# Seven pairs of gates in seven half-size products ahead of the branch steps of a decoder layer

## The chip, the cores and the metric

The kernel runs on one core of one Trainium2 chip. The metric is device time in microseconds of one execution, the median of several. Before the change it is 1901.4 us (three runs, 1900.49 to 1901.96). A core has five engines that run side by side, each with its own queue of instructions in a fixed order: PE (matmul), DVE (vector), ACT (activation), POOL and SP, which here only issues DMAs. A matmul of this kernel takes weights of 128x128 and a moving operand of 128x512; PSUM holds eight accumulators of 128x512.

## The reference, cut to what matters

One decoder layer over 1024 tokens of width 1024, float32. The part around the change:

```
u = x * (1.0 + scale_m) + shift_m
proj = jnp.einsum('btd,de->bte', u, w_in)
...
qa, ka, va, qb, kb, vb, ga, gb = jnp.split(proj, offs, axis=-1)
...
ya = jnp.einsum('bte,ed->btd', oa.reshape(Bn, T, A_Q_W), w_branch_a)
yb = jnp.einsum('bte,ed->btd', ob.reshape(Bn, T, B_OUT_W), w_branch_b)
merged = jax.nn.sigmoid(ga) * ya + jax.nn.sigmoid(gb) * yb
return jnp.einsum('btd,de->bte', merged, w_o)
```

`oa` and `ob` are the outputs of two attentions. `scale_m`, `shift_m` and four more vectors come from `silu(c)` times `w_ada` (the adaLN work). A normalisation, a SwiGLU feed-forward (FFN) and a second normalisation follow.

## The kernel before, in words

Everything is held with features on partitions, in chunks of 128. Matmul operands are split in a high and a low part (`split`, L116: ACT copies to a rounded format, DVE subtracts), and each product is made of three matmuls, high x high, high x low, low x high (`mac`, L136, lines 137 to 139). Each engine issues its instructions in the order in which the program emits them (L107), so a waiting instruction holds all that are queued behind it on its engine.

- **u**, the modulated input, is kept split in eight tiles of `bigu` (L127 to 133): for each part, token half t and half of the features.
- **Weights** come through `class Weights` (L41): three raw pieces of 128x512 loaded ahead by SP, split into four pairs of buffers; `take` hands out pieces in the order of `add`, `prepare` and `step` split the next ones.
- **Phase 1** (to L776): projections of u and the two attentions, interleaved. Two gate chunks, `tail_gates` (L149), are made at its end and written to `ga_d` (L697 to 700). Attention outputs go to `oa_d` (eight tiles of 128x1024, the last one by POOL's queue, L618 to 625) and `ob_d`.
- **Branch phase** (L781 to 915). The order is written out in `order` (L159 to 164): 24 branch steps, three branches of eight chunks, each step 24 matmuls from four attention parts; and the 14 remaining gates, each 48 matmuls from u (`make_gate`, L850): one ahead of step 0, which belongs to step 8, and then one ahead of each step from 8 to 22, save those made early, which are only loaded. `o_parts` (L804) loads four attention parts through two buffers and splits them, at the gates ahead of steps 0, 8 and 16. `merge` (L863) puts a step's result in `merged`: ACT copies in branch 0, DVE adds and POOL multiplies by the gate in branch 1, DVE multiplies and POOL adds in branch 2. `split_merged` splits the result for the output projection.
- **adaLN work**: `ada_steps` (L815) is a generator that is advanced by one at each branch step and three or four times in each gate. It makes the vectors 2, 3, 4 and 5: for each, eight rows of `w_ada` are loaded (512 KB each) and summed on DVE (L824, L826), then some matmuls with ones finish it (L835 or L842).
- **FFN** (from L1039): the first product of gate and up weights is made as seven half-size products per pair of chunks (Strassen's scheme): operands `b11`, `b21`, `t2`, `t1`, `t3`, `b22`, `t4` are sums and differences of blocks of the input, and the weights' sums are made on POOL (`g_sums`, L1073). `product` (L1100, matmuls at L1106) is 12 matmuls. The first two products of three pairs need only `b11` and `b21`, and run while the other operands are being made (`late_input`, L1149).

Of the kernel before, what the change touches and what calls it, by code (L numbers as in the profile page):

```python
# [10 lines left out]
F32 = mybir.dt.float32  # L11
# [7 lines left out]
P = 128  # L19
# [77 lines left out]

@with_exitstack
def decoder_layer(ctx: ExitStack, tc: tile.TileContext, I, out, dbg=None):
# [27 lines left out]
    def wide(name, pool, halves=(0, 1)):  # L127

        ts = {(s, t, k): pool.tile([P, 4, TH], F32R, name=f"{name}{s}{t}{k}", tag="big")
              for t in halves for k in range(2) for s in range(2)}  # L130
        return lambda s, t, k: ts[s, t, k // 4][:, k % 4]

    u = wide("u", bigu)
# [18 lines left out]
    for dc in tail_gates:  # L152
        add_chunk(I["w_in"][46 + dc], 2, 4)
    steps = [(b, dc) for b in range(3) for dc in range(KC)]
    gate_of = {8 + dc: 46 + dc for dc in range(KC)}
    gate_of.update({16 + dc: 54 + dc for dc in range(KC)})
    branch_w = [I["w_branch_a"][0], I["w_branch_a"][1], I["w_branch_b"]]
    made_early = [8 + dc for dc in tail_gates]
    order = []  # L159
    for i in range(len(steps)):  # L160
        g = 8 if i == 0 else i + 1
        if g in gate_of and i != 7:
            order.append(("g", g))
        order.append(("w", i))
    for kind, i in order:
        if kind == "g" and i not in made_early:
            add_chunk(I["w_in"][gate_of[i]], 2, 4)
        elif kind == "w":
            b, dc = steps[i]
            add_chunk(branch_w[b][dc], 1, 4)  # L170
# [37 lines left out]
    oa_d = dram.tile([A_PAIRS, P, T], F32, name="oa_d")  # L208
    ob_d = dram.tile([B_PAIRS, P, T], F32, name="ob_d")
    ga_d = dram.tile([KC, P, T], F32, name="ga_d")  # L210
# [7 lines left out]
    with tc.tile_pool(name="pro", bufs=2) as pro:  # L218
# [38 lines left out]
        def modulate(j):  # L257
            mod = pro.tile([P, 2], F32, name="mod", bufs=3)
# [521 lines left out]

    zp = ctx.enter_context(tc.tile_pool(name="zp", bufs=2, side="right", reuse_waits="tile"))  # L781
    misc = ctx.enter_context(tc.tile_pool(name="misc", bufs=1, side="right", reuse_waits="tile"))
    pools["low"] = low = ctx.enter_context(tc.tile_pool(name="low", bufs=6, reuse_waits="tile"))
    ph2b = ExitStack()
    mix = ph2b.enter_context(tc.tile_pool(name="mix", bufs=2, reuse_waits="tile"))
# [18 lines left out]
    def o_parts(b):  # L804
        parts = []
        for k in range(4):
            send_parts(4 * b + 4)
            hl = low.tile([P, 2, T], F32R, name="o_hl", tag="big")
            split(hl[:, 0], hl[:, 1], o_raws.pop(0))
            parts.append(hl)  # L810
        return parts

    shsc = misc.tile([P, 2, KC], F32, name="shsc")

    def ada_steps():  # L815
        for m in (2, 3, 4, 5):
            acc = mix.tile([P, T], F32, name="acc", bufs=1)
            raws = {}
            for k in range(KC + 1):
                if k < KC:  # L820
                    raws[k] = mix.tile([P, T], F32, name="a_raw", bufs=2)
                    nc.sync.dma_start(raws[k], I["w_ada"][k * P:(k + 1) * P, m * D:(m + 1) * D])
                if k == 1:
                    nc.vector.tensor_scalar(acc, raws[0], c_act[:, 0:1], None, op0=OP.mult)  # L824
                elif k > 1:
                    nc.vector.scalar_tensor_tensor(acc, raws[k - 1], c_act[:, k - 1:k], acc, op0=OP.mult, op1=OP.add)  # L826
                yield
            yield
            if m in (2, 5):
                gt = (mix if m == 2 else misc).tile([P, T], F32, name=f"gate{m}", bufs=1)  # L830
                nc.sync.dma_start(gt, I["b_ada"][:, m * D:(m + 1) * D].to_broadcast([P, D]))
                for t in range(2):
                    s = slice(t * TH, (t + 1) * TH)
                    ps = ps_2.tile([P, TH], F32, name="p2")
                    nc.tensor.matmul(ps, ones, acc[:, s], start=True, stop=True)  # L835
                    nc.vector.tensor_tensor(gt[:, s], ps, gt[:, s], op=OP.add)
                nc.vector.tensor_scalar(gt, gt, 1.0, None, op0=OP.add)
                gates[m] = gt
            else:
                ps = ps_2.tile([P, TH], F32, name="p2")  # L840
                for k in range(KC):
                    nc.tensor.matmul(ps[:, k:k + 1], acc[:, k * P:(k + 1) * P], ones[:, :1], start=True, stop=True)  # L842
                nc.vector.tensor_tensor(shsc[:, m - 3], ps[:, :KC], b_pp[:, m * 8:m * 8 + 8], op=OP.add)
                if m == 4:
                    nc.vector.tensor_scalar(shsc[:, 1], shsc[:, 1], 1.0, None, op0=OP.add)

    ada = ada_steps()
    gts = {}

    def make_gate(i, *steps):  # L850
        g = mix.tile([P, T], F32, name="gt", bufs=2)
        gts[i] = g
        if i in made_early:
            nc.sync.dma_start(g, ga_d[i - 8])
            return
        ps = [ps_2.tile([P, TH], F32, name="p2") for _ in range(2)]
        for n, t in enumerate(gemm_u(ps, ws.take(2), *steps)):
            if n % 4 == 2:
                next(ada, None)
            if t is not None:  # L860
                sigmoid_half(g[:, t * TH:(t + 1) * TH], ps[t])
# [551 lines left out]
```

## Time and profile before

| what | value |
|---|---|
| median of three runs | 1901.4 us |
| the profiled execution, its own time | 1908.77 us |
| its span, first to last instruction | 1907.0 us |
| granted TensorE clock over the span | 0.987 |
| gates and branches, from the first gate matmul to the output projection | 819.80 to 1122.24 us |
| gate matmuls (`p<-u`) in this stretch | 3 x 224 |
| branch matmuls (`p<-o_hl`) in this stretch | 3 x 192 |
| adaLN sums on DVE, L826 | x28, 1323 ns each |
| half-size products of the FFN, L1106 | 21 groups of 88 matmuls, the first at 1217.4 us |

The page gives busy time by engine, a strip of 40 slices, the DMA queues and the costliest groups of instructions. In a group's line stand line, engine, operation, the written and read tiles by name, the shape, the count; then busy us and mean ns of one; then the idle time of the engine just before them and what ended it. Matmuls are pipelined, so that their durations overlap. A row of windows gives for one stretch each engine's busy time with the count of its instructions, then granted clock, DMA share and GB/s. A row of the timeline gives start, duration, engine, line and, in brackets, the engine's idle time before it and what released it.

### The profile page before, as it was taken

The page shows a single profiled execution, that of the slowest core. Times are in us where ns is not written, and L with a number is a line of the kernel's source. Part 1 is how long each engine was busy: PE and PEld are TensorE (multiplying, and loading weights), DVE is VectorE, ACT ScalarE, POOL GpSimd, SP SyncE. Part 2 cuts the span into 40 slices and gives each one's busy share as a digit, 9 for nine tenths or more (in the row PEclk, how much of TensorE's full clock was granted, in tenths as well). Part 3 has the DMA queues.
Part 4 walks back from the last instruction along what each step waited for, and adds up shares of the span by engine and source line. Part 5 has one row for each costly group of instructions (what it writes and reads, how often), then busy time and mean ns, then how long its engine had stood idle before and what let it go on. Part 6 is the DMA issues. An engine that isn't in the chain of part 4 may idle for free.

```text
span 1907.0 us, 24471 instructions
## 1 busy us (share of the span) xinstructions
PE 1841.1 (97%) x8988; PEld 1489.6 (78%) x8988; DVE 1160.4 (61%) x2161; ACT 782.0 (41%) x1661; POOL 596.5 (31%) x389
## 2 busy tenths in 40 slices
PE   6899999999999999989999999999999999899998
PEld 5688877878878777768888878778888888788886
DVE  7855667667677887534555364575565444565557
ACT  3455545445444767633122132653333333412122
POOL 2432223223323222100311142455664333431213
PEclk9899999999999999989999999999999999999999
DMA  8011112111121122254534123123222222432222
GB/s 316 28 34 34 40 41 74 45 57 56 41 63 50 53 89 68 79 178 164 175 118 161 56 75 124 56 89 100 89 78 89 78 89 95 135 125 90 93 71 89
DMA packets 72266, 170.83 MB, mean 90 GB/s; under 512 B 13073, under 2 KB 14161, under 8 KB 72146
## 3 DMA queue, kind: packets, MB, share of 16 engines
q1 hardware_dynamic: 71810, 168.21, 26.7%
q8 instruction: 71, 1.16, 0.3%
q0 software_dynamic: 336, 1.06, 0.2%
q14 instruction: 49, 0.40, 0.1%
HBM read 145.80 MB, written 23.43 MB: 89 GB/s over the span
## 4 chain that ended last, share of the span: by engine, by line
PE 51%; DVE 3%; ACT 1%; issue 1%; DMA 1%; SPq 0%; POOL 0%; DVEq 0%; ACTq 0%; POOLq 0%
PE pf L1106 21%; PE p L138 5%; PE p L139 5%; PE p L137 5%; PE pf L137 5%; PE pf L139 5%; PE pf L138 5%; DVE m L118 1%; DMA h_raw<-h_d 0%; DVE wd L79 0%; DVE h L118 0%; DMA oa_d<-o 0%; PE px L1034 0%; PE p L835 0%; PE p L842 0%
## 5 line engine op out<-in xcount | busy, mean ns | idle before, releaser
L137 PE MATMUL pj<-u,w_hi 128*128 128x512 f32 x720 | 301.5, 419 | 0.0
L139 PE MATMUL pj<-u,w_lo 128*128 128x512 f32 x720 | 283.9, 394 | 0.0
L138 PE MATMUL pj<-u,w_hi 128*128 128x512 f32 x720 | 282.6, 392 | 0.0
L425 POOL TENSOR_TENSOR rb<-rb,sin_t 128x512 f32<-128x512 f32 x64 | 86.8, 1356 | 502.0 <-DVE rb L423 431.5
L118 DVE TENSOR_TENSOR w_lo<-r,w_hi 128x512 fp32r<-128x512 f32 x110 | 117.7, 1072 | 138.7 <-ACT w_hi L117 137.9
L79 DVE TENSOR_TENSOR w_lo<-w_raw,w_hi 128x512 fp32r<-128x512 f32 x150 | 133.4, 893 | 85.3 <-ACT w_hi L78 83.0
L528 ACT ACTIVATE probs<-probs,st 128x128 f32<-128x128 f32 (+1 forms) x320 | 146.0, 461 | 60.5 <-DVE st L518 30.8
L137 PEld LDWEIGHTS pj<-u,w_hi 128*128 128x128 f32 x720 | 136.4, 189 | 33.6 <-issue 4.7
L139 PEld LDWEIGHTS pj<-u,w_lo 128*128 128x128 f32 x720 | 135.8, 189 | 30.7
L138 PEld LDWEIGHTS pj<-u,w_hi 128*128 128x128 f32 x720 | 136.7, 190 | 22.6
L137 PE MATMUL pf<-wd,h 128*128 128x512 f32 x352 | 139.2, 395 | 3.4 <-DVE zt L1326 2.9
L138 PE MATMUL pf<-wd,h 128*128 128x512 f32 x352 | 138.7, 394 | 1.9 <-DVE wd L79 1.9
L139 PE MATMUL pf<-wd,h 128*128 128x512 f32 x352 | 138.6, 394 | 0.0
L62 POOL TENSOR_TENSOR w_raw<-w_raw,gate 128x512 f32<-128x512 f32 x60 | 83.1, 1404 | 157.0 <-DMA w_raw<-in_w_down 134.4
L1326 DVE SCALAR_TENSOR_TENSOR zt<-zt,pf 128x512 f32<-128x512 f32 x112 | 76.2, 685 | 85.1 <-PE pf L139 85.0
L426 POOL TENSOR_TENSOR r<-ra,rb 128x512 f32<-128x512 f32 x63 | 114.5, 1817 | 6.1 <-DVE kl L460 1.3
L78 ACT ACTIVATE w_hi<-w_raw 128x512 fp32r<-128x512 f32 x150 | 92.0, 624 | 29.0 <-PE p L138 12.0
L552 ACT ACTIVATE ptsb<-pt 128x512 f32<-128x512 f32 (+1 forms) x128 | 63.6, 548 | 93.6 <-PE pt L550 93.2
L137 PE MATMUL p<-u,w_hi 128*128 128x512 f32 x224 | 88.3, 394 | 0.0
L139 PE MATMUL p<-u,w_lo 128*128 128x512 f32 x224 | 87.2, 389 | 0.0
L138 PE MATMUL p<-u,w_hi 128*128 128x512 f32 x224 | 87.2, 389 | 0.0
L137 PE MATMUL p<-o_hl,w_hi 128*128 128x512 f32 x192 | 75.9, 395 | 8.0 <-ACT o_hl L117 8.0
(297 smaller groups left out, 4267.2 us busy)
## 6 DMA issues: line engine op xcount, KB each, us to landing
w_raw<-in_w_in SPq DMA_DIRECT2D x118, 256.0 KB
r<-in_w_gate_up SPq DMA_DIRECT2D x47, 512.0 KB
a_raw<-in_w_ada SPq DMA_DIRECT2D x32, 512.0 KB
w_raw<-in_w_down SPq DMA_DIRECT2D x44, 256.0 KB
h_raw<-h_d SPq DMA_DIRECT2D x22, 512.0 KB
h_d<-g SPq DMA_DIRECT2D x40, 256.0 KB
wa<-in_w_ada_m SPq DMA_DIRECT2D x16, 512.0 KB
wb<-wt_d SPq DMA_DIRECT2D x24, 256.0 KB
```

What stands on the lines that cost most here:

```text
L62: self.nc.gpsimd.tensor_tensor(self.raws[i], self.raws[i], scale(), op=OP.mult)
L78: self.nc.scalar.activation(hi, raw, AF.Copy)
L79: self.nc.vector.tensor_tensor(lo, raw, hi, op=OP.subtract)
L118: nc.vector.tensor_tensor(lo, src, hi, op=OP.subtract)
L137: nc.tensor.matmul(ps, w[0], m[0], start=first, stop=False)
L138: nc.tensor.matmul(ps, w[0], m[1], start=False, stop=False)
L139: nc.tensor.matmul(ps, w[1], m[0], start=False, stop=last)
L425: eng.tensor_tensor(b, b, sin_t[:, s], op=OP.mult)
L426: eng.tensor_tensor(residue_half(res, r, t), by_residue(a, r), by_residue(b, r), op=OP.add)
L528: nc.scalar.activation(pr, pr, AF.Exp, bias=st[:, 0, h, b:b + 1], accum_out=st[:, 1, h, b:b + 1])
L1106: nc.tensor.matmul(ps, w[:, c], m[:, k], start=first and k == 0 and n == 0, stop=k == 3 and n == 2, skip_group_check=True)
L1326: nc.vector.scalar_tensor_tensor(z, z, ALPHA if gi == 0 else 1.0, pd, op0=OP.mult, op1=OP.add)
```

## The change

The 14 gates leave the branch steps. A phase of their own follows phase 1 and precedes all branch steps:

- The 14 gate chunks form seven pairs, each computed by the FFN's scheme in seven products of 12 matmuls. The FFN's helpers become a class, `SevenProducts`, which both phases use.
- `b11`, `b21` and `b22` are tiles of u that exist already. `t1`, `t2`, `t3` and `t4` need differences in float32, so the input is loaded again (`u_load`, 1 MB for each of four slices), scaled again on ACT with the vectors that are now kept in `mods`, subtracted on POOL and DVE, and split (`u_differences`).
- The first two products of four pairs run first. Their weights: those of pairs 0 and 1 through `Weights`, those of pairs 2 and 3 by a load of their own. Then come the other products of those pairs and the three remaining pairs.
- Each gate is put together from the products on ACT, DVE and POOL, goes through the sigmoid and is written to `ga_d`; the branch steps load all 16 gates from there.
- Of the adaLN work the vectors 3 and 4 (22 advances of the generator) are made in this phase, 2 and 5 in the branch steps.
- In the branch steps the attention parts of the next branch are loaded and split one by one at steps 3 to 6 of the branch before, branch 1's into `bigu`; those of branch 0 are all loaded and split ahead of step 0. `merged` is split one chunk a step from step 17 on. `oa_d` becomes eight tensors.

The core of the diff:

```diff
-        add_chunk(I["w_in"][gate_of[i]], 2, 4)
+    for p in range(2):
+        add_chunk(I["w_in"][pairs[p][0]], 2, 4)
...
+    def product(self, ps, i, first):
+        hi, lo = self.ready.pop(0)
+        b = self.B[PRODUCTS[i]]
+        for k in range(4):
+            c = slice(k * P, (k + 1) * P)
+            for n, (w, m) in enumerate(((hi, b[0]), (hi, b[1]), (lo, b[0]))):
+                self.nc.tensor.matmul(ps, w[:, c], m[:, k], start=first and k == 0 and n == 0,
+                                      stop=k == 3 and n == 2, skip_group_check=True)
...
+    def u_load(k):
+        again[k] = [row(), row()]
+        for x_t, j in zip(again[k], (k, k + 4)):
+            nc.sync.dma_start(x_t, I["xT"][j])
+
+    def u_differences(k):
+        ua, ub = again.pop(k)
+        for x_t, j in ((ua, k), (ub, k + 4)):
+            nc.scalar.activation(x_t, x_t, AF.Identity, bias=mods[:, j, 0:1], scale=mods[:, j, 1:2])
+        t3 = raw_t3[k // 2][:, (k % 2) * TH:(k % 2 + 1) * TH]
+        nc.gpsimd.tensor_tensor(t3, ub[:, t_half], ua[:, t_half], op=OP.subtract)
+        nc.vector.tensor_tensor(ua[:, t_half], ua[:, t_half], ua[:, :TH], op=OP.subtract)
+        nc.vector.tensor_tensor(ua[:, :TH], ub[:, t_half], ua[:, t_half], op=OP.subtract)
+        nc.vector.tensor_tensor(ub[:, :TH], ub[:, :TH], ua[:, :TH], op=OP.subtract)
+        for name, src in (("t2", ua[:, :TH]), ("t1", ua[:, t_half]), ("t4", ub[:, :TH])):
+            split_to(name, k, src)
...
+    def first_quarter(p):
+        dst = out_half(pairs[p][0], 0)
+        nc.scalar.activation(dst, acc[p][0], AF.Copy)
+        nc.vector.tensor_tensor(dst, dst, acc[p][1], op=OP.add)
+        gate_out(pairs[p][0], 0)
+
+    ws.prepare(4)
+    for got in ws.done[ws.used:ws.used + 4]:
+        gat.ready.append(got[:2])
+    ws.used += 4
+    u_load(0)
+    for p in (2, 3):
+        gat.load(p, False)
+    u_load(1)
+    for p in range(EARLY_GATES):
+        acc[p] = [ps_2.tile([P, TH], F32, name="p2") for _ in range(2)]
+        for i in range(2):
+            gat.product(acc[p][i], i, True)
+            if p < 2:
+                gat.split(2 + p, i)
+        u_differences(p)
+        if p + 2 < 4:
+            u_load(p + 2)
+        if p < 2:
+            gat.load(p)
+        first_quarter(p)
+        if p == 2:
+            for step in range(3):
+                gat.sums(0, step)
+    operand("t3", bigu)
+    gat.jobs = [(p, i) for p in range(len(pairs)) for i in range(2 if p < EARLY_GATES else 0, 7)]
+    gat.prepare(2)
+    for k in range(4):
+        split_to("t3", k, raw_t3[k // 2][:, (k % 2) * TH:(k % 2 + 1) * TH])
...
+    send_parts(2)
...
+    for k in range(4):
+        o_part(0, k)
+    for i, (b, dc) in enumerate(steps):
+        w = ws.take(1)
...
+        if b < 2 and dc >= 3 and dc < 7:
+            o_part(b + 1, dc - 3)
+        if i + 1 >= 8 and i + 1 < len(steps):
+            make_gate(i + 1)
```

Here `gate_out` is the sigmoid (ACT tanh, then a scaling on DVE) and, once both halves are done, the write to `ga_d`; `make_gate` is now only the load; `o_part` splits one attention part and has the next one loaded.

More of the change, by code (lines that the diff above doesn't have):

```diff
@@ new lines, in decoder_layer @@
+    again = {}
+    def u_load(k):
[13 more added lines that the diff above has]
+            split_to(name, k, src)
@@ new lines, in mrg, with send_parts, o_part @@
+    def mrg(dc, t):
+        return merged[dc // 4][:, dc % 4, t * TH:(t + 1) * TH]
+    o_src = [oa_d[p] for p in range(A_PAIRS)] + [ob_d[p] for p in range(B_PAIRS)]
+    o_raws, o_sent = [], [0]
+    def send_parts(upto):
+        while o_sent[0] < min(upto, len(o_src)) and len(o_raws) < 2:
+            raw = mix.tile([P, T], F32, name="o_raw", bufs=2)
+            nc.sync.dma_start(raw, o_src[o_sent[0]])
+            o_raws.append(raw)
+            o_sent[0] += 1
+    parts_of = {}
+    def o_part(b, k):
+        send_parts(4 * b + k + 1)
+        hl = (bigu if b == 1 else low).tile([P, 2, T], F32R, name="o_hl", tag="big")
+        split(hl[:, 0], hl[:, 1], o_raws.pop(0))
+        parts_of.setdefault(b, []).append(hl)
+        send_parts(len(o_src))
@@ L848, in decoder_layer, with make_gate @@
     gts = {}
-    def make_gate(i, *steps):
+    def make_gate(i):
         g = mix.tile([P, T], F32, name="gt", bufs=2)
         gts[i] = g
[L853 to L861, printed above, removed]
+        nc.sync.dma_start(g, ga_d[i - 8])
```

277 lines of the change are left out of this document (149 added, 128 removed).

## The prediction

> **What bounds the kernel now.** I read the page first, then the stage between the last tail gate and the output projection by windows, then its PE groups, then single instructions.
>
> ```profile
> span 1907.0 us, 24471 instructions
> PE 1841.1 (97%) x8988; PEld 1489.6 (78%) x8988; DVE 1160.4 (61%) x2161; ACT 782.0 (41%) x1661; POOL 596.5 (31%) x389
> ```
>
> The profiled execution's own time is 1908.8 us, 7.4 above the median of 1901.4; I work out a difference in the profile and apply it to the median. About 0.2% (4 us) is what a measurement of this kernel can tell from no change.
>
> ```profile
> core 0: us, PE busy (x) PEld busy (x) DVE busy (x) ACT busy (x) POOL busy (x), PEclk, DMA share, GB/s
> 819.80:830.77 10.97, 10.97 (x49) 9.10 (x50) 3.04 (x5) 2.89 (x5) 1.72 (x3) 1.00 0.87 280
> 830.77:886.52 55.75, 46.94 (x194) 37.65 (x192) 18.91 (x21) 16.80 (x28) 2.95 (x2) 0.91 0.47 161
> 886.52:1122.24 235.72, 235.72 (x1050) 194.30 (x1048) 118.82 (x147) 51.87 (x89) 51.52 (x32) 1.00 0.37 122
> 1260.00:1640.00 380.00, 380.00 (x1678) 314.74 (x1678) 205.51 (x222) 147.46 (x263) 188.07 (x121) 1.00 0.27 90
> 822.00:830.00 8.00, 8.00 (x37) 6.63 (x36) 1.27 (x2) 1.06 (x1) 1.03 (x2) 1.00 0.97 298
> ```
>
> ```profile
> L137 PE MATMUL p<-u,w_hi 128*128 128x512 f32 x224 | 88.3, 394 | 0.0
> L137 PE MATMUL p<-o_hl,w_hi 128*128 128x512 f32 x192 | 75.9, 395 | 8.0 <-ACT o_hl L117 8.0
> ```
>
> The first window is one gate, the second the eight steps of branch 0, the third everything else up to the projection, the fourth the FFN's seven-product phase, which runs for 380 us without a hole. PE is the bound in all of them. A matmul lasts 394 ns, but these overlap: 380.00 us over 1678 is **0.2265 us from start to start**, and that, not 394 ns, is what a removed matmul is worth. Eight branch steps are 192 matmuls, 43.5 us at that spacing, and took 55.75: 12.3 us are lost in branch 0 before.
>
> ```profile
> 842.32 0.80 PE L137 MATMUL p<-o_hl,w_hi 128*128 128x512 f32 x1 [8.00 <-ACT o_hl L117]
> 843.58 0.80 PE L138 MATMUL p<-o_hl,w_hi 128*128 128x512 f32 x1 [0.46 <-DVE o_hl L118]
> 845.03 0.63 PE L138 MATMUL p<-o_hl,w_hi 128*128 128x512 f32 x1
> 845.45 0.63 PE L139 MATMUL p<-o_hl,w_lo 128*128 128x512 f32 x1
> 848.39 0.39 PE L137 MATMUL p<-o_hl,w_hi 128*128 128x512 f32 x1
> ```
>
> That loss is one hole of 8.0 us (the third and fourth attention part come late), and then matmuls 0.42 us apart until 848.39: from 843.58 on eleven distances from start to start take 4.81 us where 2.49 are due. So a long hole costs 2.3 us more after it ends. The granted clock of the window, 0.91, shows the same.
>
> **The products.** Fourteen gates are 224 x 3 = 672 matmuls of 128x512. Seven pairs in seven products of 12 are 588 of the same shape. 84 fewer at 0.2265 us: **-19.0 us**. The adaLN matmuls and the 576 of the branches stay.
>
> The Trainium skill, "TensorE: Matmul & The Clock Gate", section "Back-to-back issue gap", gives about 131 ns for each matmul in a sustained stream of load-and-matmul pairs at 512 columns; by that the 84 would be worth 11.0 us, an estimate. The window of 380 us disagrees, and the measurement decides.
>
> **The old hole.** Branch 0 now comes more than 130 us after the attention's last write, so that write can no longer hold it: **-12.3 us**.
>
> **The early gates.** The new phase opens with 8 products that need only the old u: 96 matmuls, 21.7 us, from 819.8 to 841.5. Then PE needs t2, all four slices, and the weights of pair 0's third product. Those hang on a chain through ACT, DVE and POOL, each in the order of emission. Per slice k: two scalings of 128x1024 on ACT; POOL subtracts for t3; DVE may overwrite that half of x only after POOL has read it, then makes three differences, each from the one before; ACT writes three high parts, DVE three low parts; then the gate's first quarter: ACT copy, DVE add, ACT tanh. The next slice's scaling is queued on ACT behind that tanh, so slices don't overlap.
>
> ```profile
> L265 ACT ACTIVATE ut<-xt,mod x9: 802/1239/1247, 11.3 to 64.2; 128x1024 f32<-128x1024 f32 x7, 128x512 f32<-128x512 f32 x2
> L1047 POOL TENSOR_TENSOR b11l<-raw,b11h x4: 1293/1298/1303, 1202.2 to 1209.9; 128x512 fp32r<-128x512 f32 x4
> L1163 POOL TENSOR_TENSOR r<-r x3: 1807/1810/1814, 1225.6 to 1233.6; 128x512 f32<-128x512 f32 x3
> L1155 DVE TENSOR_TENSOR raw<-r,raw x3: 677/678/692, 1224.7 to 1232.7; 128x512 f32<-128x512 f32 x3
> L1156 DVE TENSOR_TENSOR raw_t<-r,raw x3: 691/692/693, 1225.5 to 1233.5; 128x512 f32<-128x512 f32 x3
> L1047 DVE TENSOR_TENSOR t2l<-raw_t,t2h x4: 999/1002/1003, 1226.9 to 1239.2; 128x512 fp32r<-128x512 f32 x4
> L1047 DVE TENSOR_TENSOR t1l<-raw,t1h x4: 677/678/679, 1231.5 to 1240.7; 128x512 fp32r<-128x512 f32 x4
> ```
>
> ```profile
> L78 ACT ACTIVATE w_hi<-w_raw 128x512 fp32r<-128x512 f32 x150 | 92.0, 624 | 29.0 <-PE p L138 12.0 <-POOL w_raw L62 10.9 <-PE p L139 5.5
> L681 ACT ACTIVATE gt<-p 128x512 f32<-128x512 f32 x28 | 16.5, 596 | 154.6 <-PE p L139 136.1 <-issue 9.3 <-DVE acc L826 9.2
> L1260 DVE TENSOR_TENSOR g<-g,pf 128x512 f32<-128x512 f32 x40 | 27.5, 687 | 15.5 <-PE pf L1106 15.5
> ```
>
> Scalings 2.4 (two of 1.24, slightly overlapped), POOL 1.3 (1.8 where DVE works beside it), two differences with hand-over 1.4, three high parts from there on 1.7 (the third difference lies beneath), last low part 0.8, add 0.7, tanh 0.6: 8.9, with the hops **9.0 us per slice**. Between 8.5 and 10.
>
> Where it starts: SP sends the tail gate's result, two branch weights, x^T for slice 0 (1 MB), then the first half-weights of pairs 2 and 3. ACT's next job is the split of pair 2's, queued ahead of slice 0.
>
> ```profile
> 821.25 1.72 SPq L800 DMA_DIRECT2D o_raw<-oa_d  x2
> ```
>
> ```profile
> 827.82 1.06 ACT L117 ACTIVATE o_hl<-o_raw 128x1024 fp32r<-128x1024 f32 x1 [6.44 <-DMA o_raw<-oa_d]
> 830.53 1.06 ACT L117 ACTIVATE o_hl<-o_raw 128x1024 fp32r<-128x1024 f32 x1 [1.64 <-DMA o_raw<-oa_d]
> ```
>
> ```profile
> 833.86 2.35 POOL L624 TENSOR_TENSOR o<-o,vt 128x1024 f32<-128x1024 f32 x1 [7.49 <-issue]
> 836.50 0.60 POOL L625 DMA_DIRECT2D oa_d<-o  x1 [0.30 <-POOL o L624]
> ```
>
> In the same place 1 MB issued at 821.25 was in by 830.5, with the DMA 97% busy at 298 GB/s. I take 830.5 for pair 2's weights (828 to 834: half a MB more is queued ahead, but the engines stay full from 823 on). Two splits, 1.1: slice 0 at 831.6. POOL isn't free then: it still has attention's last pair (L624, L625) until 837.1, where slice 0 wants it at 834: +3.2. Slice 0 ends at 843.8. Only behind it stand pair 3's two splits on ACT (1.1), so pair 3's products wait too, from 836.5 to about 845, inside the longer wait. Slices 1 to 3: 27.0, and 1.5 for POOL's weight sums beside slice 2's DVE work (1.0 against 0.68 above): 873.4. Then pair 0's split, 0.6: **PE goes on at 874.0 instead of 841.5: +32.5**, and 2.3 for the cold clock: **+34.8**. With the bounds of start (-2.5 to +3.5), slice (-2 to +4) and POOL (-3 to +3): 27 to 43.
>
> **The steady gates** copy the FFN's scheme, which holds 0.2265 us. They add three adaLN steps a pair on DVE; DVE is 54% busy in the FFN's window (205.51 of 380) with the same splits. I cost this at nothing, up to 3.
>
> **Into the branches.** Before, a gate's 10.97 us covered the first splits and the step's weights were split ahead of them. Now nothing does. After the last product ends: ACT copy and tanh 1.2, DVE scaling 0.4, and only then can SP pass the write of that gate and issue the first two attention parts.
>
> ```profile
> 847.00 0.43 SPq L822 DMA_DIRECT2D a_raw<-in_w_ada  x1
> ```
>
> ```profile
> 850.92 1.28 DVE L826 SCALAR_TENSOR_TENSOR acc<-a_raw,c_act,acc 128x1024 f32<-128x1024 f32 x1 [0.49 <-DMA a_raw<-in_w_ada]
> ```
>
> ```profile
> L117 ACT ACTIVATE o_hl<-o_raw 128x1024 fp32r<-128x1024 f32 x12 | 12.4, 1054 | 31.6 <-DMA o_raw<-oa_d 14.0 <-DMA oa_d<-o 9.6 <-DMA o_raw<-ob_d 8.0
> L118 DVE TENSOR_TENSOR o_hl<-o_raw,o_hl 128x1024 fp32r<-128x1024 f32 x12 | 14.4, 1222 | 28.5 <-ACT o_hl L117 28.5
> ```
>
> ```profile
> L682 DVE TENSOR_SCALAR gt<-gt x28: 418/426/428, 844.6 to 1112.2; 128x512 f32<-128x512 f32 x28
> ```
>
> A load of 512 KB takes 3.9 us from issue (847.00) to landing (850.92). Issue about 2.6 after the last product, with the gate's 512 KB ahead of it: part 0 in at 6.8, split by 9.1 (1.05 + 1.22). There are two buffers, so parts 2 and 3 are issued at 9.1 and 10.2 and land at 13.0 and 14.1; part 3's high half is done at 15.2. The step's own weights are split behind all four parts: high at 15.8, low at 17.1. PE has the adaLN's matmuls until about 1.7 and then nothing until 15.8: 14.1 idle, about 0.8 more for the low weights, 2.3 cold clock: **+17.2** (12 if the loads land faster, 20 if a buffer is still held).
>
> The second half of the branches lose their gate matmuls as cover. A step is 24 matmuls, 5.44 us; DVE per step in branch 2: weights 0.7, two products from PSUM 1.4, adaLN 1.28, two low parts of the merged rows 1.4 to 2: 4.8 to 5.4. Just beneath PE; cost nothing, up to 4.
>
> **Sum**: -19.0 - 12.3 + 34.8 + 17.2 = **+20.7 us**; 1901.4 becomes **1922.1**.
>
> On the clock the same page of the Trainium skill ("What's actually happening") says that the array falls to half rate after an idle window of some 3.4 us and recovers after as long a busy one, which speaks against both new holes. By it each would cost 1.7 us, an estimate; the trace agrees on half rate (0.42 against 0.2265), at 2.3.
>
> **Rivals.**
> Not slower: the differences hide beneath the early products. Place: the same four slices; it decides at PE's return. If t2 and its weights are there by 853.3 instead of 874.0, the change is even. The FFN's similar slices start 4.0 us apart (L1155: 1224.7 to 1232.7 for three); four of those from 831.6, with POOL free at once, end at 847.6 and PE returns at 848.2: 6.7 lost and 2.3 for the clock in place of 34.8, so -19.0 - 12.3 + 9.0 + 17.2 = -5.1: 1896. For it: the FFN builds the same t operands with little loss. Against: there the scalings come out of PE, and no first quarter stands between the slices. Chance 0.13. Half of that effect gives no change: 0.06.
> Worse: the DMA becomes the bound in steps 8 to 15. They load 8 weights of 256 KB, 8 gates, 8 adaLN rows and 4 attention parts of 512 KB, 12.6 MB in 43.5 us, 290 GB/s; the busiest row shows 298. It decides below 290: at 240 these steps take 52 us, and the whole is +29: 1930. Against: loads are issued ahead by two buffers. Chance 0.10.
>
> **How the numbers follow.** The forecast has 0.71; its bounds (27 to 43, 12 to 20, 0 to 7) give 1909 to 1940. The range reaches down to 1903 for the even case and to 1938: it leaves out most of the faster rival and the tail. Faster 0.13, same 0.06, slower 0.81.
>
> **What would show it.** Right: a hole of about 20 us on PE ahead of the first t2 product, ended by ACT or DVE of w_hi and w_lo; slices 9 us apart on ACT; a shorter hole ahead of pair 3's products; 588 gate matmuls at 0.2265; a hole of about 14 us ahead of the first branch product, ended by the branch weights' split; no hole in branch 0 from attention's last write; the FFN unchanged. Wrong: PE back before 853, the branch hole under 8 us, or holes inside steps 8 to 15 ended by loads.

## The result, and the profile after

| | before | after |
|---|---|---|
| median of three runs | 1901.4 us (1900.49 to 1901.96) | **1943.81 us** (1942.89 to 1945.09) |
| ratio of the times, 95% interval | | 1.0225 [1.0209, 1.0241] |
| span of the profiled execution | 1907.0 us | 1942.0 us |
| granted TensorE clock over the span | 0.987 | 0.977 |

The change makes the kernel 42.4 us slower. The forecast was 20.7 us slower with a range up to 1938: the sign was right, the size was half of it, and the time lies above the range.

The head of the page of after:

```profile
span 1942.0 us, 24554 instructions
PE 1827.4 (94%) x8904; PEld 1475.2 (76%) x8904; DVE 1228.0 (63%) x2224; ACT 834.3 (43%) x1741; POOL 651.7 (34%) x428
```

PE has 84 instructions and 13.7 us of busy time less than before, and yet the span is longer: the time is in holes. Windows of both kernels, by stage, place it. First before: gates and branches, output projection, the FFN's products.

```profile
819.80:1122.24 302.44, 293.63 (x1290) 241.04 (x1290) 140.78 (x173) 71.55 (x120) 56.19 (x37) 0.98 0.41 135
1122.24:1168.39 46.15, 43.98 (x194) 35.80 (x192) 28.46 (x31) 12.89 (x20) 23.06 (x17) 1.00 0.36 113
1217.44:1648.32 430.88, 426.73 (x1881) 351.74 (x1880) 246.75 (x280) 181.26 (x319) 214.93 (x137) 0.99 0.26 87
```

Then the same three stages of after:

```profile
818.07:1159.27 341.20, 284.25 (x1206) 229.50 (x1206) 210.57 (x240) 124.94 (x202) 110.40 (x75) 0.91 0.53 181
1159.27:1209.36 50.09, 46.80 (x194) 37.92 (x192) 26.27 (x27) 12.14 (x19) 24.63 (x17) 0.93 0.31 104
1258.30:1688.34 430.04, 426.30 (x1882) 351.63 (x1880) 246.87 (x280) 181.28 (x319) 213.09 (x135) 0.99 0.26 87
```

Gates and branches take 38.8 us more, the output projection 3.9 us more, the FFN nothing. The span grew by 35.0 us only, less than the 42.4 of the medians: the profiled execution of before was itself 7.4 us above its median, and 5.0 of that lie behind the FFN's products, in work that the change doesn't touch (258.69 us against 253.71 after). Inside the first stage, windows of the early gates up to the first product on t2, the other gates, and the branches:

```profile
818.07:878.01 59.94, 26.10 (x97) 20.03 (x97) 27.38 (x41) 24.99 (x37) 14.28 (x12) 0.74 0.48 167
878.01:1017.01 139.00, 119.24 (x524) 97.87 (x525) 86.58 (x102) 61.09 (x105) 48.31 (x32) 0.93 0.49 167
1017.01:1159.27 142.26, 138.91 (x585) 111.60 (x585) 96.60 (x99) 38.85 (x62) 47.81 (x31) 0.97 0.59 199
```

In the first of these PE does 96 matmuls, worth 21.7 us, in 59.94. The PE rows of the timeline at the end of each larger hole say what ended it:

```profile
832.41 0.73 PE L153 MATMUL p<-u,w_hi 128*128 128x512 f32 x2 [3.19 <-ACT w_hi L176]
846.79 1.22 PE L153 MATMUL p<-u,w_hi 128*128 128x512 f32 x2 [6.79 <-ACT w_hi L176]
878.01 0.79 PE L153 MATMUL p<-t2h,w_hi 128*128 128x512 f32 x1 [23.87 <-ACT w_hi L176]
...
918.03 0.50 PE L153 MATMUL p<-t3h,w_lo 128*128 128x512 f32 x1 [4.86 <-DVE w_lo L177]
...
1017.01 0.80 PE L198 MATMUL p<-o_hl,w_hi 128*128 128x512 f32 x1 [13.94 <-ACT w_hi L78]
1152.52 0.50 PE L200 MATMUL p<-o_hl,w_lo 128*128 128x512 f32 x1 [2.58 <-DVE w_lo L79]
1168.65 0.79 PE L199 MATMUL p<-w_lo,m 128*128 128x512 f32 x1 [2.74 <-DVE w_lo L79]
```

The first three are the early gates (33.9 us), and the fifth is the entry into the branches: both stages were forecast to wait. The fourth, inside the gate loop, and the last two, in branch 2 and the output projection, were not.

### The profile page after: what moved, and what is told of

Read it like the earlier page. It is cut to its first block, busy times and chain, and to the rows that moved or that the text cites. A ratio compares the mean times of both kernels' runs of the same rounds, so it can differ in the third digit from the quotient of the medians.

```text
span 1942.0 us, 24554 instructions
## 1 busy us (share of the span) xinstructions
PE 1827.4 (94%) x8904; PEld 1475.2 (76%) x8904; DVE 1228.0 (63%) x2224; ACT 834.3 (43%) x1741; POOL 651.7 (34%) x428
## 4 chain that ended last, share of the span: by engine, by line
PE 44%; DVE 5%; DMA 2%; ACT 1%; issue 1%; POOL 0%; SPq 0%; DVEq 0%; POOLq 0%; ACTq 0%
PE pf L153 21%; PE p L153 5%; PE pf L198 5%; PE pf L199 4%; PE pf L200 4%; PE p L200 2%; PE p L199 2%; PE p L198 2%; DVE m L177 1%; DMA gate<-in_b_ada 1%; DVE w_lo L79 1%; DVE acc L864 1%; DMA a_raw<-in_w_ada 1%; DMA o_raw<-oa_d 1%; DMA h_raw<-h_d 0%
## 5 line engine op out<-in xcount | busy, mean ns | idle before, releaser
L177 DVE TENSOR_TENSOR w_lo<-r,w_hi 128x512 fp32r<-128x512 f32 x141 | 146.0, 1041 | 160.1 <-ACT w_hi L176 159.4
L79 DVE TENSOR_TENSOR w_lo<-w_raw,w_hi 128x512 fp32r<-128x512 f32 x126 | 112.5, 896 | 92.4 <-ACT w_hi L78 89.8
L78 ACT ACTIVATE w_hi<-w_raw 128x512 fp32r<-128x512 f32 x126 | 78.1, 624 | 49.8 <-POOL w_raw L62 19.0
L176 ACT ACTIVATE w_hi<-r 128x512 fp32r<-128x512 f32 x141 | 87.2, 621 | 14.4 <-DMA r<-in_w_in 12.1
L200 PE MATMUL p<-o_hl,w_lo 128*128 128x512 f32 x192 | 76.6, 399 | 3.3 <-DVE w_lo L79 3.2
L491 ACT ACTIVATE qs<-r 64x1024 fp32r<-64x1024 f32 x38 | 40.1, 1055 | 90.8 <-POOL r L478 90.4
```

What stands on the lines that cost most here:

```text
L78: self.nc.scalar.activation(hi, raw, AF.Copy)
L79: self.nc.vector.tensor_tensor(lo, raw, hi, op=OP.subtract)
L176: nc.scalar.activation(hi, src, AF.Copy)
L177: nc.vector.tensor_tensor(lo, src, hi, op=OP.subtract)
L200: nc.tensor.matmul(ps, w[1], m[0], start=False, stop=last)
```

## The experiments

All numbers are medians beside the kernel before on the same chip, which took 1900.15 us (kernels 1 to 4), 1900.48 (5 to 8) and 1900.61 (9 to 12). The changed kernel was not run again beside them: a gain against it compares two sessions, in which the kernel before differs by about 1 us, and the runs of one kernel spread over 0.6 to 9 us. So a gain of 1.8 us (kernel 5) is not clear of noise, and those of 4.8 and 4.9 (kernels 6 and 9) are good to about 2 us, an estimate from these spreads; they rest on the rows shown beside them. The theory after the result: five separate waits, each with its own cause. The main rival: one shared resource (DVE's load), so that a cure at one place shows as a wait at the next.

### 1. No operand chain (a part of the computation left out)

The second load of x, the scalings, differences and splits are gone; tiles of u stand in for t1 to t4.

```diff
-    for name, pool in (("t2", low), ("t1", low), ("t4", low)):
-        operand(name, pool)
+    for name, old in (("t2", "b11"), ("t1", "b21"), ("t4", "b22"), ("t3", "b11")):
+        B[name] = B[old]
...
-    u_load(0)
...
-        u_differences(p)
```

> Leaves out the second load of the input, its scaling, the differences and the operands t1 to t4; tiles of the old u stand in their place, so that all matmuls, weights, loads of weights and evacuations stay. Theory A (the chain of slices on ACT, DVE and POOL holds PE for 24 us ahead of the first t2 product): PE goes on at about 844, as soon as POOL has made pair 0's weight sums, in place of 878.0, and the cold clock behind the hole is gone; the time falls from 1943.8 by 35 to 40 us to about 1906. Rival B (the weights of the first pairs, loaded and split late, hold PE): the hole ahead of the first t2 product stays over 15 us and the time stays above 1925.

Measured: **1906.11 us**, 37.7 less than the changed kernel, ratio to before 1.0026 [1.0016, 1.0037]. The chain costs 37.7 us. What is left of the loss lies elsewhere, and is more than the 6.0 us by which this kernel is still above the one before: the saved matmuls and the old hole (31.3 us) pay for other waits.

### 2. The queues of the early gates reordered

Scaling, differences and splits of the slices are emitted interleaved, and the first quarters follow behind them. Slice 0's subtraction for t3 goes from POOL to DVE as well.

```diff
-        u_differences(p)
-        if p + 2 < 4:
-            u_load(p + 2)
...
-        first_quarter(p)
...
+    u_scale(1)
+    u_subtract(1)
+    u_split(0)
+    u_load(3)
+    u_scale(2)
+    u_subtract(2)
+    u_split(1)
...
+    for p in range(1, EARLY_GATES):
+        first_quarter(p)
```

> Does the same work in another order: scaling of slice k+1 is queued ahead of the splits of slice k, the first quarters of the gates come behind all slices, pair 3's weights are split ahead of the slices, and the first slice's subtraction for t3 is on DVE, not on POOL. Theory A' (it is the order in the queues that makes the chain long): PE goes on at about 857 in place of 878.0, time about 1923. Rival B' (the amount of work on ACT and DVE, or the landing of x, sets it): PE goes on after 870, time above 1936.

Measured: **1934.53 us**, ratio 1.0178 [1.0162, 1.0193]. Two PE rows of its timeline:

```profile
862.78 0.79 PE L153 MATMUL p<-t2h,w_hi 128*128 128x512 f32 x1 [14.26 <-ACT row L936]
...
877.94 0.79 PE L153 MATMUL p<-t3h,w_hi 128*128 128x512 f32 x1 [7.12 <-ACT row L1003]
```

The product on t2 begins 41.5 us into the phase instead of 59.9, so the order of emission, with that one subtraction, was worth 18.4 us there. But the first quarters put behind the slices now hold ACT, and the product on t3 waits 7.12 us for a copy out of its bank (L1003). So 9.3 us are left of the 18.4, half of what was expected.

### 3. adaLN steps only beside products

In the changed kernel the condition for a step of the adaLN generator also holds where a product has been done early and gives PE no work, if the count n of products is even there. That is so at the first two products of pair 2, right behind the step at the end of pair 1: three in a row. The edit also lets the steps begin with pair 0.

```diff
-            if p and n % 2 == 0 and ada_pools["work"] is gp and len(ada_count) < 22:
+            if (p, i) in gat.jobs and n % 2 == 0 and ada_pools["work"] is gp and len(ada_count) < 22:
```

> Advances the adaLN generator only behind a product, from pair 0 on, in place of three advances in a row at the seam of pairs 1 and 2. Theory A (three rows of w_ada in a row with two buffers hold DVE, and the low weights behind them, so PE has the hole of 4.9 us at 912.8 and a cold clock): this hole goes, 5 to 8 us less, about 1937. Rival B (the DMA is too busy there, whatever the order): the hole stays and the time is within 2 us of 1943.8.

Measured: **1934.72 us** (1932.66 to 1936.81), ratio 1.0179 [1.0164, 1.0194]: 9.1 us for one condition, where 5 to 8 were expected. From the first product on t2 to the first branch matmul the profile has 133.02 us instead of 139.00, 6.0 less; no row shown here places the rest. At the place of the hole of 4.86 us its PE row says:

```profile
912.32 0.50 PE L153 MATMUL p<-t3h,w_lo 128*128 128x512 f32 x1 [0.66 <-DVE w_lo L177]
```

### 4. The first attention parts split beside the last pair's products

```diff
+            if p == len(pairs) - 1:
+                if i == 0:
+                    send_parts(2)
+                if i in (2, 3, 4, 5):
+                    o_part(0, i - 2)
+                if i == 5:
+                    ws.prepare(1)
...
-    for k in range(4):
-        o_part(0, k)
```

> Loads the four attention parts of branch 0 from the last pair's first product on, splits them behind products 3 to 6 of the last pair, and splits the first branch weights there too. Theory A (the hole of 13.9 us ahead of the branches is the chain load, split, load, split, weights): it falls below 3 us with no cold clock behind it, 13 to 16 us less, about 1929. Rival B (ACT and DVE are full there, so the work only moves): holes of the same size appear ahead of the last products, time within 4 us of 1943.8.

Measured: **1934.12 us**, ratio 1.0176 [1.0161, 1.0191]. Two PE rows:

```profile
1006.35 0.37 PE L880 MATMUL p<-ones,acc 128*128 128x1 f32 x1 [4.34 <-DVE acc L864]
...
1009.79 0.77 PE L198 MATMUL p<-o_hl,w_hi 128*128 128x512 f32 x1
```

The branches' first matmul no longer waits. The last adaLN steps are queued on DVE behind the parts, and their matmuls wait 4.34 us: 9.7 us gained where 13 to 16 were expected.

### 5. adaLN of the branches done early

```diff
             if n == 3:
                 ws.step()
+                if 1 <= i <= 6:
+                    next(ada, None)
```

> The adaLN work of the branches runs two steps at once in branch steps 1 to 6, so that it is over by about step 16 and VectorE's step in branch 2 loses its 1.27 us multiply-add, 6.08 to 4.8 us, beneath TensorE's 5.44. Theory (the load of VectorE in branch 2 costs about 10 us, in the branch stage and carried into W_o): about 1934, 8 to 10 us below the changed kernel. Rival (these are waits for the row of biases alone, or a loss that TensorE makes up later): 1941 to 1944. Second rival (the doubled loads in steps 1 to 6 hold up the weights): 1944 or more.

Measured: **1942.05 us**, ratio 1.0219 [1.0203, 1.0234]. My theory fell here, and the time lies where the first rival put it (1941 to 1944). The multiply-adds are gone from branch 2, and the output projection still begins with the same hole (2.73 us, ended by DVE's low part of its weights). What branch 2 gains is lost in steps 5 to 7. There DVE stands still ahead of the adaLN gate's sum, as a row of its timeline shows; the row of biases that this sum reads was issued at 1055.37 us, when the wait began, so I take the wait to be for that load, though the row names PE (kernel 9 takes the load up):

```profile
1060.73 1.29 DVE L874 TENSOR_TENSOR gate<-p,gate 128x512 f32<-128x512 f32 x2 [5.76 <-PE p L200]
```

### 6. Branch 2's add on DVE instead of POOL

```diff
-            nc.gpsimd.tensor_tensor(m, m, tmp, op=OP.add)
+            nc.vector.tensor_tensor(m, m, tmp, op=OP.add)
```

> The add that closes branch 2's merge goes from GpSimd to VectorE: two more instructions of about 0.69 us in each of the last eight steps. Theory (the low parts of merged rows take 1.58 us instead of 0.69 because GpSimd's add reads memory beside them): they fall to about 0.69, VectorE's step goes from 6.08 to about 5.7 us, and the time falls by 1 to 4 us, to about 1941. Rival (VectorE's durations are its own and its load is what counts): the step becomes 7.4 us, about 2 us above TensorE's in each of six or seven steps, and the time rises by 8 to 12 us, to about 1954.

Measured: **1938.98 us**, ratio 1.0204 [1.0189, 1.0220]: 4.8 us less with sixteen instructions *more* on DVE; 1 to 4 were expected. DVE's groups of 1112 to 1170 us, by shape, in the changed kernel:

```profile
L177 DVE TENSOR_TENSOR m<-zt,m 128x512 fp32r<-128x512 f32 x16 | 25.5, 1638 | 0.0
L1049 DVE TENSOR_TENSOR gy<-p,gt 128x512 f32<-128x512 f32 x16 | 10.3, 682 | 0.8 <-DMA gt<-ga_d 0.7
```

and in this one:

```profile
L177 DVE TENSOR_TENSOR m<-zt,m 128x512 fp32r<-128x512 f32 x16 | 11.3, 753 | 0.0
L1050 DVE TENSOR_TENSOR zt<-zt,gy 128x512 f32<-128x512 f32 x16 | 11.1, 693 | 1.5
```

The low parts of the merged rows fall from 25.5 to 11.3 us, and the adds cost 11.1: DVE is rid of more than it takes on. The product from PSUM (L1049) lasted 0.68 us beside POOL too; only the low part, whose two inputs both lie in SBUF, was slowed. The output projection's window shrinks from 50.09 to 44.42 us.

### 7. All of it together

The four edits of 2 to 5; in the early gates all differences and the first sums on DVE, the t3 parts earlier, the quarters of pairs 1 to 3 in the loop; the 22 adaLN steps spread evenly.

```diff
-        nc.gpsimd.tensor_tensor(t3, ub[:, t_half], ua[:, t_half], op=OP.subtract)
+        nc.vector.tensor_tensor(t3, ub[:, t_half], ua[:, t_half], op=OP.subtract)
...
+            if i == 5 and p + 1 < EARLY_GATES:
+                first_quarter(p + 1)
```

> All four edits together, with the queues of the early gates in a better order: the differences and the first sums on VectorE alone, the parts of the third product ahead of the rest, and the quarters of pairs 1 to 3 only in the loop. Theory (the losses are separate and add up: about 9 for the burst of adaLN steps, 13 for the branch entry, 8 to 10 for branch 2, and 17 to 20 of the 38 us of the early gates): about 1896, 1890 to 1902, near the time before the change. Rival (the losses share one resource, so that each cure moves the wait on): 1910 to 1925.

Measured: **1915.98 us**, ratio 1.0083 [1.0068, 1.0098]. The time lies in the rival's range and not in the theory's. The gain is 27.8 us; kernels 2 to 5 alone gained 9.3, 9.1, 9.7 and 1.8, 29.9 together. That this nearly adds up speaks for separate waits, but does not show them: this kernel has further edits in the early gates, and kernels 2 and 4 had each moved a part of their wait on (7.12 and 4.34 us). The expectation of 1896 used the sizes that I had hoped for instead of the four measured ones; with those it would have been about 1914. The row at the first product on t2 shows what is left:

```profile
859.74 0.80 PE L153 MATMUL p<-t2h,w_hi 128*128 128x512 f32 x1 [13.79 <-ACT w_hi L176]
```

### 8. One pair as two plain gates, as cover

Six pairs in seven products; the seventh pair's 96 matmuls, which need only the old u, run between the early products (now of three pairs) and the first product on t2.

```diff
-    EARLY_GATES = 4
+    EARLY_GATES = 3
+    pairs = pairs[:PLAIN]
...
+    def plain_products(g):
+        w = [gat.ready.pop(0) for _ in range(2)]
+        plain_ps[g] = [ps_2.tile([P, TH], F32, name="p2") for _ in range(2)]
+        for t in range(2):
+            for k in range(8):
+                kh, c = k // 4, slice((k % 4) * P, (k % 4 + 1) * P)
+                mac(plain_ps[g][t], [x[:, c] for x in w[kh]], [u_tiles[x, t, kh][:, k % 4] for x in range(2)], k == 0, k == 7)
```

> As the seventh, but only six pairs in seven products, and the last pair's two gates as plain products of 48 matmuls each between the first quarters of pairs 0 to 2 and the third product: 16.3 + 21.7 = 38 us of TensorE work ahead of it instead of 21.75, where the third product could start 41.5 us into the phase with the reordered queues. It gives back 2.7 us of the products. Theory (the early hole is only a lack of work that does not need the differences): 10 to 15 us below the seventh kernel, about 1884, 1878 to 1892, below the time before. Rival (the slices take as long as there is work beside them, since VectorE and ScalarE also split the plain gates' weights): no faster than the seventh kernel.

Measured: **1904.01 us**, ratio 1.0016 [1.0006, 1.0025]: 12.0 us below kernel 7, as the theory had it. The time itself, and "below the time before", missed: 1884 had been counted from the 1896 expected of kernel 7. The PE row of the first t2 product carries no wait any more:

```profile
861.73 0.39 PE L153 MATMUL p<-t2h,w_hi 128*128 128x512 f32 x1
```

### 9. The changed kernel with the bias rows loaded early

```diff
             raws = {}
+            if m in (2, 5):
+                gt = ada_pools[m].tile([P, T], F32, name=f"gate{m}", bufs=1)
+                nc.sync.dma_start(gt, I["b_ada"][:, m * D:(m + 1) * D].to_broadcast([P, D]))
...
-                gt = ada_pools[m].tile([P, T], F32, name=f"gate{m}", bufs=1)
-                nc.sync.dma_start(gt, I["b_ada"][:, m * D:(m + 1) * D].to_broadcast([P, D]))
```

> The changed kernel with one edit: the row of biases of an adaLN gate is loaded at the start of that gate's eleven steps instead of in the step that uses it. Theory (the part of the branch stage's loss that did not go with GpSimd's add is VectorE's wait for this row, at the end of branch steps 10 and 22, 1.8 and 2.4 us of TensorE's spacing in those steps): 2 to 4 us less, about 1941. Rival (GpSimd's add holds VectorE up by then anyway): within 1 us of the changed kernel.

Measured: **1938.87 us**, ratio 1.0197 [1.0183, 1.0210], 4.9 less, where 2 to 4 were expected. The gain is not where I expected it: the two steps in which an adaLN gate is finished (10 and 21, counted from 0) keep their 1.3 and 2.0 us above a plain step. It is in the last step of branch 2. DVE's row there in the changed kernel, and the last step's window:

```profile
1149.85 1.29 DVE L874 TENSOR_TENSOR gate<-p,gate 128x512 f32<-128x512 f32 x2 [3.74 <-DMA gate<-in_b_ada]
...
1149.34:1159.27 9.93, 7.35 (x26) 5.56 (x24) 7.55 (x10) 1.35 (x3) 4.67 (x3) 0.83 0.24 79
```

and the same window with the rows loaded early:

```profile
1147.54:1152.97 5.43, 5.43 (x25) 4.36 (x24) 3.39 (x4) 0.72 (x2) 4.68 (x3) 1.00 0.46 145
```

DVE stood 3.74 us behind a load issued only 7.1 us before (at 1142.72), the low part of the last step's own weights was queued behind it (L79, the hole of 2.58 us at 1152.52), and with the cold clock that followed PE lost 4.5 us. In the kernel before, DVE waited 4.26 us for the same load, in a stretch in which PE was busy without a hole (886.52 to 1122.24 us):

```profile
1061.49 1.29 DVE L836 TENSOR_TENSOR gate<-p,gate 128x512 f32<-128x512 f32 x2 [4.26 <-DMA gate<-in_b_ada]
```

### 10. The best of it

Kernel 8 without the doubled adaLN steps of kernel 5, with the edits of 6 and 9, pair 1's sums on DVE, and the adaLN steps from the sixth product on.

```diff
-                gat.sums(p + 1, i - 2)
+                gat.sums(p + 1, i - 2, nc.vector.tensor_tensor if p == 0 else None)
```

> The eighth kernel without its doubled adaLN steps in the branches, with branch 2's add and the first two pairs' sums on VectorE, the biases loaded early, and the 22 adaLN steps of the gate phase spread from the sixth product on. Theory (the losses add: 4.8 for the add, about 4 for the seam of the branches, 2 to 4 for the start of the loop): about 1893, 1888 to 1897, below the time before by 0.2 to 0.6%. Rival (VectorE becomes the bound of the gate loop, since it takes the sums over): 1898 or more.

Measured: **1890.42 us** (1889.63 to 1890.67), ratio to before 0.9942 [0.9930, 0.9953]: faster than both kernels, by 10.2 and 53.4 us, and within the range expected. Its windows of the early gates, the other gates and the branches:

```profile
817.06:859.32 42.26, 39.59 (x170) 31.15 (x170) 27.50 (x41) 20.87 (x30) 6.50 (x6) 1.00 0.72 262
859.32:973.05 113.73, 105.97 (x464) 84.89 (x464) 83.02 (x106) 57.38 (x102) 35.39 (x23) 0.98 0.55 183
973.05:1108.17 135.12, 134.51 (x584) 109.73 (x585) 94.75 (x114) 40.41 (x64) 29.96 (x19) 1.00 0.65 216
```

Gates and branches take 291.11 us, 11.3 less than before. The saved matmuls (72 at 0.2265 us: 16.3) and the old hole (12.3) could give 28.6, so some 17 us of small waits are left.

### 11. Only 11 adaLN steps beside the gates

```diff
-    while len(ada_count) < 22:
+    while len(ada_count) < 11:
...
+                if i <= 8:
+                    next(ada, None)
```

> As the tenth, but only 11 adaLN steps in the gate phase; the other 33 go to the branches, two in each of steps 0 to 8. Theory (in the gate loop VectorE is within a few us per pair of TensorE's 19.0 us, and stands in the way with adaLN's multiply-adds beside GpSimd's sums): 2 to 5 us below the tenth, about 1890. Rival (the loop has room, and the doubled loads of 512 KB delay the branch steps): 2 to 5 us above it.

Measured: **1894.91 us**, ratio 0.9968 [0.9957, 0.9979], 4.5 above kernel 10, as the rival had it. At its place the theory holds too. Windows of its gate loop and its branches:

```profile
863.39:966.03 102.64, 100.50 (x450) 82.58 (x448) 73.69 (x95) 57.07 (x100) 33.31 (x23) 1.00 0.47 162
966.03:1114.38 148.35, 141.18 (x600) 113.10 (x601) 105.61 (x122) 40.48 (x64) 30.17 (x19) 0.98 0.67 225
```

Against kernel 10 the loop gains 11.1 us, a part of which is adaLN's matmuls that left it, and the branches lose 13.2. Another 1.9 us lie in the early gates (44.15 against 42.26), up to whose end the two programs are the same; why they differ there is not known.

### 12. No POOL in the gate loop

```diff
-        tt = self.nc.gpsimd.tensor_tensor
+        tt = self.nc.vector.tensor_tensor
...
-                nc.gpsimd.tensor_tensor(out_half(eb, 1), kept.pop(4), kept.pop(3), op=OP.add)
+                nc.vector.tensor_tensor(out_half(eb, 1), kept.pop(4), kept.pop(3), op=OP.add)
```

> As the tenth, with all sums and the add of the gate loop on VectorE, so that GpSimd does nothing in it: five more instructions of 0.69 us for VectorE in each pair's 19.0 us. Theory (GpSimd's instructions cost VectorE as much by slowing it as they save): equal to the tenth or up to 4 us below. Rival (VectorE's number of instructions is what counts): 3 to 10 us above the tenth.

Measured: **1894.95 us** (1891.02 to 1900.13), ratio 0.9969 [0.9958, 0.9979]: 4.5 above kernel 10, the rival's side. DVE's low parts of the weights in the gate loop of kernel 10:

```profile
L177 DVE TENSOR_TENSOR w_lo<-r,w_hi 128x512 fp32r<-128x512 f32 x24 | 24.9, 1048 | 4.9 <-DMA r<-in_w_in 3.3 <-ACT w_hi L176 1.6
```

and without POOL:

```profile
L177 DVE TENSOR_TENSOR w_lo<-r,w_hi 128x512 fp32r<-128x512 f32 x24 | 16.5, 687 | 4.4 <-ACT w_hi L176 4.2
```

They are faster by a third, and DVE's busy time in the loop is the same as before the move, 82.76 us in 127 instructions against 83.02 in 106: so far the theory holds. In branch 2 the same move saved 14.2 us of low parts for 11.1 us of adds; here it only breaks even. Why the loop still comes out 1.9 us longer (115.63 against 113.73) is open. Another 2.7 us of the difference lie in the early gates (44.99 against 42.26), up to whose end the programs of kernels 10 to 12 are the same, so that more than half of the 4.5 us can't be laid on the edit by any row here.

## Why the prediction was right or wrong

| step of the prediction | forecast, us | from the profile of after, us | alone on the chip, us |
|---|---|---|---|
| products | -19.0 | -19.0 | |
| old hole in branch 0 | -12.3 | -12.3 | |
| early gates | +34.8 | +39.7 | 37.7 (kernel 1) |
| steady gates | 0 | +6.7 | 9.1 (kernel 3) |
| entry into the branches | +17.2 | +16.2 | 9.7, with a new hole of 4.34 (kernel 4) |
| branch 2 and projection | 0 | +9.8 | 4.8 (kernel 6), 4.9 (kernel 9) |
| sum | +20.7 | +41.1 | (medians: +42.4) |

The windows of gates, branches and projection are 42.7 us longer together; the 1.6 us that the table lacks are smaller differences, the largest of them a wait of 0.90 us for an adaLN sum at 1001.12 us.

**Products and old hole: right.** PE has exactly 84 instructions less, steps 1 to 7 of branch 0 take 5.44 us each, and the FFN's stage is unchanged.

**Early gates: mechanism right, 5 us too small.** ACT's rows, from pair 2's split over the four slices' scalings to pair 0's split:

```profile
831.73 1.15 ACT L176 ACTIVATE w_hi<-r 128x512 fp32r<-128x512 f32 x2 [12.08 <-DMA r<-in_w_in]
832.79 2.36 ACT L904 ACTIVATE row<-row,mods 128x1024 f32<-128x1024 f32 x2
...
842.99 0.63 ACT L843 ACTIVATE t1h<-row 128x512 fp32r<-128x512 f32 x1 [1.61 <-DMA oa_d<-o]
...
847.16 2.36 ACT L904 ACTIVATE row<-row,mods 128x1024 f32<-128x1024 f32 x2
...
856.32 2.36 ACT L904 ACTIVATE row<-row,mods 128x1024 f32<-128x1024 f32 x2
...
868.37 2.36 ACT L904 ACTIVATE row<-row,mods 128x1024 f32<-128x1024 f32 x2
...
877.35 1.14 ACT L176 ACTIVATE w_hi<-s 128x512 fp32r<-128x512 f32 x2
```

Undisturbed slices take 9.16 and 8.98 us, forecast 9.0. The weights landed 1.2 us later than I took, slice 0 lost 1.1 us more (its second high part waited for attention's last write, which I had not seen), and slice 2 took 12.05 us instead of 10.5. The phase began 1.7 us earlier. DVE's first difference of slice 1, its three differences of slice 2, and POOL's three weight sums beside those:

```profile
850.91 0.69 DVE L907 TENSOR_TENSOR row<-row 128x512 f32<-128x512 f32 x1 [2.86 <-POOL row L906]
...
860.10 1.73 DVE L907 TENSOR_TENSOR row<-row 128x512 f32<-128x512 f32 x1 [3.23 <-POOL row L906]
861.94 1.56 DVE L908 TENSOR_TENSOR row<-row 128x512 f32<-128x512 f32 x1
863.54 1.65 DVE L909 TENSOR_TENSOR row<-row 128x512 f32<-128x512 f32 x1
...
860.03 1.26 POOL L123 TENSOR_TENSOR s<-r 128x512 f32<-128x512 f32 x1
861.37 1.59 POOL L125 TENSOR_TENSOR s<-s,r 128x512 f32<-128x512 f32 x1
862.92 1.71 POOL L127 TENSOR_TENSOR r<-r,r 128x512 f32<-128x512 f32 x1
```

Beside the sums each difference took 1.56 to 1.73 us instead of 0.69; I had allowed 1.0, by a row of the FFN. Each ends 0.54 to 0.56 us after the sum beside it has ended, as if it did most of its work only then.

**Steady gates: the step that failed first.** "I cost this at nothing, up to 3." The seven-product scheme does hold its pace, but I counted three adaLN steps a pair as if they were spread. At the seam from pair 1 to pair 2 three fall together, since the first two products of pair 2 are already done and give no time for them. DVE's rows there:

```profile
909.36 2.31 DVE L864 SCALAR_TENSOR_TENSOR acc<-a_raw,c_act,acc 128x1024 f32<-128x1024 f32 x1
914.55 1.28 DVE L864 SCALAR_TENSOR_TENSOR acc<-a_raw,c_act,acc 128x1024 f32<-128x1024 f32 x1 [2.88 <-DMA a_raw<-in_w_ada]
916.09 1.28 DVE L864 SCALAR_TENSOR_TENSOR acc<-a_raw,c_act,acc 128x1024 f32<-128x1024 f32 x1 [0.26 <-DMA a_raw<-in_w_ada]
917.29 1.29 DVE L177 TENSOR_TENSOR w_lo<-r,w_hi 128x512 fp32r<-128x512 f32 x2
```

There are two buffers for the rows, so that the loads of the next two could be issued only from 909.90 us on, while DVE waits, and the weights that PE needs stand behind it in DVE's queue: a hole of 4.86 us and a cold clock, 6.7 in all.

**Entry: right.** 13.94 us idle, forecast 14.1, ended by the branch weights' split as forecast; step 0 then takes 2.2 us above 5.44, against 3.1 for low weights and clock.

**Branch 2: failed.** "Just beneath PE; cost nothing, up to 4." I summed DVE's step to 4.8 to 5.4 us, with 1.4 to 2 for two low parts. They took 3.3 (1638 ns each), the step 6.1, against PE's 5.44: steps 19 to 22 lost 1.4 us, the last one 4.5, the projection 3.9. Kernel 6 shows that POOL's add makes the difference in the low parts and the projection, kernel 5 that relieving DVE of other work does not cure the projection's part of it. The 4.5 us of the last step are the bias row's load (kernel 9): in the kernel before, a wait of 4.26 us for it cost PE nothing, among the gates' matmuls; I listed the adaLN rows and not this load. I had written that these steps "lose their gate matmuls as cover", and by that both belonged in the sum.

The Trainium skill, "SBUF — State Buffer", section "SBUF: two separate sides", says that VectorE with two SBUF inputs and a GpSimd operation that reads SBUF exclude each other, so that the second waits for the whole of the first. The runs agree: 1638 ns beside POOL's add and 753 without it, differences that end just after POOL's sums, and no slowing of L1049 (682 ns), whose one input is in PSUM. That page would have spoken against "just beneath".

**The rivals.** "Not slower" needed PE back by 853.3; it was back at 878.01. DMA as the bound did not occur: steps 8, 9 and 12 to 15 of after take 5.44 us. The range was too narrow above, since two terms set to nothing were given 3 and 4 us and cost 6.7 and 9.8. Besides, the bounds named for the early gates (+3.5, +4, +3 on 34.8) add up to 45.3 and not to 43, so that the sum's own upper end was 1942 and not 1940, and the range stopped at 1938.

## What to carry to other kernels

When a phase loses the long matmul block that stood beside it, every load, split and generator step that the block covered needs a new cover, and the sum must list each of them; here a saving of 19 us ended as a loss of 42, because most of them had none. Work that needs none of the new operands (here two plain gates, 2.7 us dearer) made a good cover: with it, a spread of the side work, the bias rows loaded early and branch 2's add on DVE the same scheme came out 0.6% faster than before. An engine that is "just beneath" the bound in a sum of undisturbed durations should be priced again with the durations it has beside POOL.

## What the runs showed of the hardware

- DVE subtractions of 128x512 with both inputs in SBUF take 0.69 us alone, 1.56 to 1.73 beside POOL's sums and 1.64 in the mean beside its adds; beside the sums they ended 0.54 to 0.56 us after POOL did. DVE products with one input in PSUM keep 0.68.
- Moving work from POOL to DVE can make DVE's own total smaller: in branch 2 16 adds of 693 ns came, and 16 low parts lost 885 ns each. In the gate loop it left the total as it was (83.02 and 82.76 us) and the kernel no faster.
- The product after the hole of 23.87 us took 1.5 us more than its due, with the granted clock at 0.74 over the early gates; in the kernel before it was 2.3 us after a hole of 8.0 us. The longer hole did not cost more after its end.
